# Turning the last unit's results sooner, and issuing the last store from ScalarE

## The chip, the cores and the metric

The kernel runs on one core of one Trainium2 chip. The metric is the device time of one execution in microseconds (us), median of the runs. Besides the times there is one profiled execution with a trace of every engine: TensorE (PE, with its weight loads as PEld), VectorE (DVE), ScalarE (ACT), GpSimd (POOL) and SyncE (SP), which issues most of the DMAs. L1656 means line 1656 of the kernel.

## What is computed

One layer of a streaming encoder, for 512 prompt frames and 64 sample frames together (576 rows, 2048 wide). The attention and convolution parts do not bear on the change. It ends with a gated feed-forward block:

```python
def hybrid_layer(x, ...):
    hn = rmsnorm(x, g_norm1)
    proj = hn @ w_in
...
    x = x + mix @ w_out
    h2 = rmsnorm(x, g_norm2)
    x = x + (jax.nn.silu(h2 @ w_gate) * (h2 @ w_up)) @ w_down
    return x, k, v, new_conv
```

The change lies in the last lines' product with `w_down` (5632 x 2048): in how its last result leaves the core.

## The kernel before

**Layout.** Activations are kept with channels on the 128 partitions and the 576 frames along the free axis, in two halves of 288 frames (`HALVES`). The outputs are wanted frame by frame, so every result block (128 channels x 288 frames) is turned before it is stored.

**Products.** Each float32 matrix is split into a high and a low part in the type fp32r, and a product is three matmuls. The large products are cut 2 x 2 and computed by seven block products (numbers 1 to 7 in `run`) in place of eight. A *unit* is one such set. One pair of input blocks, three matmuls, is one *step*: after each step `pipe.tick()` is called.

**Pipeline.** Side work is written as Python generators and handed to a small heap (`Pipeline`). `yield 9` in a worker means that it goes on nine steps later. A worker that is spawned after a product first runs at the next step, so `yield 9` ahead of the work puts it ten steps behind the addition. In the down projection the order of the instructions of all engines is kept as the program text gives it (`manual_schedule`, lines 119 and 1677).

**Down units.** `DOWN` lists 37 units. The last one (number `NU - 1`) treats columns 4 of 8 (d = 4) and four pairs, so each of its products is 4 steps, 12 matmuls. Its products come in the order 1, 2, 6, 7, 5, 4, 3. Four result blocks `acc[d, c, i]` are finished by them (c: which 128 columns, i: which half of the frames):

- acc 21045 (c 0, i 0) after product 2: ScalarE copies a partial sum (L428), VectorE adds the product (L450), GpSimd adds the partial sum (L452).
- acc 21048 (c 1, i 1) after product 5: ScalarE copies (L428), GpSimd adds (L452).
- acc 21047 (c 1, i 0) after product 4: VectorE adds (L450).
- acc 21046 (c 0, i 1) after product 3, the last one: VectorE adds (L450).

**Stores.** For all units but the last, `store_blocks` turns the block on VectorE in 32 x 32 tiles (L1607) and stores it in four to six DMAs from SyncE (L1613, L1615). For the last unit `store_y` has a worker: three transposes on TensorE into a PSUM bank `pot` (L1644; `misc` gives two banks in turn), two copies back on ScalarE (L1647 for 256 frames, L1653 for the other 32), then the stores: for the first half of the frames one DMA from SyncE (L1656), for the second half an L1635 for each 128 frames, cut at frame 512 into L1635 and L1637 (prompt and sample output). The last 32 frames go out from GpSimd.

**Lanes.** The program's framework gives every DMA of SyncE or ScalarE one of eight counting semaphores, DMAHW0 to DMAHW7, here called lanes. They are given out in turn, in the framework's own order of the instructions. A DMA adds 16 to its lane when it has landed, and before it is issued its engine waits until the lane has the count that all earlier users of that lane leave behind. An engine's DMAs are issued in its program order.

Of the kernel before, what the change touches and what calls it, by code (L numbers as in the profile page):

```python
# [16 lines left out]
P = 128  # L17
TP = 512
# [84 lines left out]
def tile_hybrid_stream_step(  # L103
# [6 lines left out]
    nc = tc.nc  # L110
# [5 lines left out]
    yp, ys = y_prompt[0], y_sample[0]  # L116
# [24 lines left out]
    def misc(name):  # L141
        return ps_z.tile([P, 512], F32, tag="misc", name=name, bufs=2)
# [99 lines left out]
    rows = {}  # L242
# [1298 lines left out]
    first, last = {v[0] for v in visits.values()}, {v[-1] for v in visits.values()}  # L1541
# [55 lines left out]
    def store_blocks(n, c, i):  # L1597
        d = UNITS[n][1]
        src, c0, f0 = acc[d, c, i], (2 * d + c) * P, HALVES[i][0]
        n_p = min(HALF, TP - f0)  # L1600

        def work():
            yield 9
            if not spare:
                spare.extend(down["pool"].tile([P, HALF], F32, tag=f"ob{k}", name="ob") for k in range(2))
            ob = spare.pop(0)
            nc.vector.transpose(out=ob, in_=src)  # L1607
            spare.append(src)
            yield 5
            for k in range(P // BK):  # L1610
                rows = ob[k * BK : (k + 1) * BK, :n_p].rearrange("j (t c) -> j t c", c=BK)
                cg = slice(c0 + k * BK, c0 + (k + 1) * BK)
                nc.sync.dma_start(out=yp[f0 : f0 + n_p, cg].rearrange("(t j) c -> j t c", j=BK), in_=rows)  # L1613
            for a in range(n_p, HALF, BK):
                nc.sync.dma_start(out=ys[a - n_p : a - n_p + BK, c0 : c0 + P].rearrange("j (g c) -> g j c", c=BK),  # L1615
                                  in_=ob[:, a : a + BK])

        pipe.spawn(work())
# [3 lines left out]
    def store_y(n, c, i):  # L1622
        if n < NU - 1:
            store_blocks(n, c, i)
            return

        d = UNITS[n][1]
        src, cs, f0 = acc[d, c, i], slice((2 * d + c) * P, (2 * d + c + 1) * P), HALVES[i][0]
        r = HALF - 2 * P

        def put(f, ap, queue=nc.sync):

            rows, n_p = ap.shape[0], max(min(TP - f, ap.shape[0]), 0)
            if n_p:
                queue.dma_start(out=yp[f : f + n_p, cs], in_=ap[:n_p])  # L1635
            if n_p < rows:
                queue.dma_start(out=ys[f + n_p - TP : f + rows - TP, cs], in_=ap[n_p:])  # L1637

        def work():
            yield 9  # L1640
            po = misc("pot")[:, : 3 * P]
            for q in range(3):
                w = min(P, HALF - q * P)
                nc.tensor.transpose(po[:w, q * P : (q + 1) * P], src[:, q * P : q * P + w], ident)  # L1644
            yield 3
            ob = src[:, : 2 * P].rearrange("p (i c) -> p i c", c=P)
            nc.scalar.copy(out=ob, in_=po[:, : 2 * P].rearrange("p (i c) -> p i c", c=P))  # L1647
            if len(rests) % 2 == 0:
                rests.append(spare.pop(0))
            else:  # L1650
                rests.append(rests[-1])
            obs = rests[-1][:r, : P] if len(rests) % 2 else rests[-1][:r, P : 2 * P]
            nc.scalar.copy(out=obs, in_=po[:r, 2 * P :])  # L1653
            yield 4
            if i == 0:
                nc.sync.dma_start(out=yp[: 2 * P, cs].rearrange("(i p) c -> p i c", p=P), in_=ob)  # L1656
            else:
                put(f0, ob[:, 0, :])
                put(f0 + P, ob[:, 1, :])
            put(f0 + 2 * P, obs, nc.gpsimd if n == NU - 1 else nc.sync)  # L1660

        pipe.spawn(work())


# [80 lines left out]
```

## Time and profile before

| what | us |
|---|---|
| median of 3 runs | 2329.69 |
| lowest and highest | 2328.64, 2332.22 |
| the profiled execution's own time | 2329.59 |
| its span, first to last instruction | 2327.9 |
| PE busy | 2315.9 (99%) |
| DVE busy | 1956.4 (84%) |
| ACT busy | 1221.5 (52%) |
| POOL busy | 298.1 (13%) |
| start of the last DMA issue | 2325.38 |

Times in the trace count from the start of the span. The columns of a timeline are: start, duration, engine, line, operation, output<-input, how many, and in brackets how long the engine was idle before and what released it. A row may merge several instructions of one group; its duration then goes from the first start to the last end. SPq rows are DMA issues of SyncE: the time is that of the issue, not that of the transfer. Ends of matmuls are modelled.

### The profile page before, as it was taken

What the parts mean: (1) busy time and instruction counts of PE and PEld (TensorE: products, weight loads), DVE (VectorE), ACT (ScalarE), POOL (GpSimd) and SP (SyncE); (2) the same over time, 40 slices, a digit from 0 to 9 for tenths busy, and PEclk for the clock granted to TensorE, in tenths of its full rate; (3) what the DMA queues carried; (4) which work ended last, traced back from release to release, by engine and by line L of the source; (5) the groups of instructions that cost most, each with busy time, mean ns of one, the idle gap of its engine ahead of it and who ended that gap; (6) DMA issues with size and microseconds to landing.
All of it is one profiled execution on the core that took longest, in us unless ns stands there. A gap on an engine that the chain in (4) does not pass through costs nothing.

```text
span 2327.9 us, 43552 instructions
## 1 busy us (share of the span) xinstructions
PE 2315.9 (99%) x17432; PEld 2306.7 (99%) x17432; DVE 1956.4 (84%) x2871; ACT 1221.5 (52%) x2170; POOL 298.1 (13%) x374
## 2 busy tenths in 40 slices
PE   9999999999999999999999999999999999999999
PEld 8999999999999999999999999999999999999999
DVE  8889989897777898888888888888888777887897
ACT  8556656456887564444444444444444444444443
POOL 0211121110332320000000000000000002431222
PEclk9999999999999999999999999999999999999999
DMA  8444343546643454444444444345344936885654
GB/s 272 136 118 130 91 142 109 145 131 209 192 144 108 162 204 127 155 139 140 150 134 150 133 146 155 116 152 158 116 155 136 349 129 211 222 242 186 205 137 100
DMA packets 533770, 368.57 MB, mean 158 GB/s; under 512 B 70278, under 2 KB 518016, under 8 KB 533568
## 3 DMA queue, kind: packets, MB, share of 16 engines
q1 hardware_dynamic: 527072, 356.45, 48.9%
q0 software_dynamic: 6384, 9.21, 2.2%
q8 instruction: 136, 2.23, 0.4%
q14 instruction: 66, 0.54, 0.1%
q10 hardware_dynamic: 112, 0.14, 0.0%
HBM read 285.52 MB, written 80.23 MB: 157 GB/s over the span
## 4 chain that ended last, share of the span: by engine, by line
PE 93%; ACT 3%; DVE 2%; DMA 1%; issue 0%; POOL 0%; SPq 0%; POOLq 0%; ACTq 0%; DVEq 0%
PE psy L405 47%; PE psw L405 23%; PE psx L405 12%; PE pjo L224 6%; PE pj L691 1%; PE pjz L691 1%; PE psv L405 1%; PE pjm L691 1%; DMA raw_a<-in_w_down_dram 0%; ACT ph L228 0%; PE psx L556 0%; ACT whi L176 0%; DVE whl L229 0%; DMA raw_b<-in_w_down_dram 0%; DMA vtok<-v_dram 0%
## 5 line engine op out<-in xcount | busy, mean ns | idle before, releaser
L229 DVE TENSOR_TENSOR whl<-raw_a,whl 128x1024 fp32r<-128x1024 f32 (+4 forms) x384 | 432.8, 1128 | 55.0 <-ACT whl L228 53.4
L405 PE MATMUL psy<-t,whl 128*128 128x288 f32 x3000 | 447.2, 294 | 0.0
L228 ACT CAST whl<-raw_a 128x1024 fp32r<-128x1024 f32 (+4 forms) x384 | 360.0, 939 | 139.9 <-PE psx L405 45.3
L405 PE MATMUL psy<-h_s,whl 128*128 128x288 f32 x2766 | 416.4, 294 | 0.6 <-ACT part L428 0.6
L405 PEld LDWEIGHTS psy<-t,whl 128*128 128x128 f32 x3000 | 414.3, 188 | 0.0
L405 PE MATMUL psw<-t,whl 128*128 128x288 f32 x2688 | 388.9, 294 | 0.0
L405 PEld LDWEIGHTS psy<-h_s,whl 128*128 128x128 f32 x2766 | 383.1, 188 | 0.9 <-ACT part L428 0.8
L405 PEld LDWEIGHTS psw<-t,whl 128*128 128x128 f32 x2688 | 366.7, 188 | 0.0
L228 ACT CAST whl<-raw_b 128x1024 fp32r<-128x1024 f32 (+5 forms) x234 | 211.4, 905 | 209.9 <-issue 71.4
L229 DVE TENSOR_TENSOR whl<-raw_b,whl 128x1024 fp32r<-128x1024 f32 (+5 forms) x234 | 253.2, 1082 | 72.7 <-ACT whl L228 71.6
L428 ACT COPY part<-psy 128x288 f32<-128x288 f32 x309 | 123.2, 399 | 346.6 <-PE psy L405 343.2
L405 PE MATMUL psx<-h_s,whl 128*128 128x288 f32 x1164 | 170.2, 294 | 0.0
L228 ACT CAST whl<-s 128x1024 fp32r<-128x1024 f32 (+5 forms) x103 | 95.3, 925 | 123.5 <-PE psw L405 116.0
L405 PEld LDWEIGHTS psx<-h_s,whl 128*128 128x128 f32 x1164 | 159.6, 188 | 0.0
L405 PE MATMUL psy<-t12a,whl 128*128 128x288 f32 x1056 | 150.5, 295 | 0.0
L405 PE MATMUL psw<-t34a,whl 128*128 128x288 f32 x1056 | 150.4, 295 | 0.0
L405 PEld LDWEIGHTS psy<-t12a,whl 128*128 128x128 f32 x1056 | 143.3, 188 | 0.4 <-ACT part L428 0.2
L405 PEld LDWEIGHTS psw<-t34a,whl 128*128 128x128 f32 x1056 | 143.5, 188 | 0.0
L1454 POOL DMA_DIRECT2D hid_dram<-form x7 | 5.2, 738 | 951.7 <-DVE form L229 944.5
L229 DVE TENSOR_TENSOR whl<-s,whl 128x1024 fp32r<-128x1024 f32 (+5 forms) x103 | 110.4, 1071 | 19.2 <-ACT whl L228 18.2
L224 PE MATMUL pjo<-mixc,whi 128*128 128x288 f32 x512 | 119.0, 300 | 0.0
L224 PE MATMUL pjo<-mixa,whi 128*128 128x288 f32 x512 | 102.8, 296 | 0.0
(565 smaller groups left out, 3920.8 us busy)
## 6 DMA issues: line engine op xcount, KB each, us to landing
hid_dram<-form SPq DMA_DIRECT2D x147, 288.0 KB
raw_a<-in_w_in_dram SPq DMA_DIRECT2D x22, 1024.0 KB
raw_b<-in_w_in_dram SPq DMA_DIRECT2D x22, 1024.0 KB
raw_b<-in_w_gate_dram SPq DMA_DIRECT2D x22, 1024.0 KB
raw_b<-in_w_up_dram SPq DMA_DIRECT2D x22, 1024.0 KB
raw_a<-in_w_gate_dram SPq DMA_DIRECT2D x22, 1024.0 KB
raw_a<-in_w_up_dram SPq DMA_DIRECT2D x22, 1024.0 KB
h_s<-hid_dram SPq DMA_DIRECT2D x10, 2016.0 KB
```

Of the source, the lines that this page charges most:

```text
L224: mm(ps, w_[:, k, csl], x_[:, a:b], start=(k == 0 and n == 0), stop=(k == nk - 1 and n == 2))
L228: cast = nc.scalar.copy(out=hi, in_=src)
L229: (lo_eng or nc.vector).tensor_tensor(out=lo, in0=src, in1=hi.bitcast(F32), op=ALU.subtract)
L405: mm(ps, whl[:, w_, j, :], x_, start=(start and j == 0 and q == 0), stop=(j == len(xs_) - 1 and q == 2), skip_group_check=True)
L428: nc.scalar.copy(out=t, in_=st["y"])
L691: mm(banks_[c][i], w3[:, kt % 8, c * P : (c + 1) * P], t[:, x_, :], start=(kt == 0 and n == 0), stop=(kt == KD - 1 and n == 2))
L1454: q.dma_start(out=hid_dram[fp][2 * n - 2 : 2 * n].rearrange("f p t -> p f t"), in_=t.bitcast(F32))
```

## The change

In `store_y` the worker's three delays become shorter (nine, three and four steps become three, one and one). So the transposes come four steps behind the addition, one product, and not ten; the copies two steps behind the transposes; the stores two behind the copies. And for the blocks with i = 1, the DMA of L1637 that closes the 128 frames from f0 + 128 goes to ScalarE's queue where c = 0, which is acc 21046, the last block of all.

```diff
-        def put(f, ap, queue=nc.sync):
+        def put(f, ap, queue=nc.sync, last=None):
 
             rows, n_p = ap.shape[0], max(min(TP - f, ap.shape[0]), 0)
             if n_p:
                 queue.dma_start(out=yp[f : f + n_p, cs], in_=ap[:n_p])
             if n_p < rows:
-                queue.dma_start(out=ys[f + n_p - TP : f + rows - TP, cs], in_=ap[n_p:])
+                (last or queue).dma_start(out=ys[f + n_p - TP : f + rows - TP, cs], in_=ap[n_p:])
 
         def work():
-            yield 9
+            yield 3
             po = misc("pot")[:, : 3 * P]
...
-            yield 3
+            yield 1
             ob = src[:, : 2 * P].rearrange("p (i c) -> p i c", c=P)
...
-            yield 4
+            yield 1
             if i == 0:
                 nc.sync.dma_start(out=yp[: 2 * P, cs].rearrange("(i p) c -> p i c", p=P), in_=ob)
             else:
                 put(f0, ob[:, 0, :])
-                put(f0 + P, ob[:, 1, :])
+                put(f0 + P, ob[:, 1, :], last=nc.scalar if c == 0 else nc.sync)
             put(f0 + 2 * P, obs, nc.gpsimd if n == NU - 1 else nc.sync)
```

TensorE, around products 7 and 5 of the last unit (psw is 7, psy is 5; pot 21045 are the transposes of the first block):

```order
-L405 MATMUL psw<-t_10084,whl 128x288 x3
-L405 MATMUL psw<-h_s_8772,whl 128x288 x3
-L405 MATMUL psw<-t_6_9981,whl 128x288 x3
-L405 MATMUL psw<-h_s_8771,whl 128x288 x3
-L405 MATMUL psy<-t_10084,whl 128x288 x3
-L405 MATMUL psy<-h_s_8772,whl 128x288 x3
 L1644 MATMUL pot<-ident,acc_21045 128x128 x2
 L1644 MATMUL pot<-ident,acc_21045 32x128
```

The block 21045 was turned in the middle of product 5; now its three transposes stand ahead of product 7, right behind product 6. In the same way those of 21048 move from behind product 3 to ahead of it. Those of 21047 and 21046 stay behind product 3.

SyncE, near the end of its program, before the change, with the lane (and engine) that each issue waits for; acc5 are blocks of column pair 5, acc2_20721 blocks of pair 7, the unit before the last:

```order
L1613 DMA out_0_dram<-acc5_21201 32x9x32 [waits DMAHW4_49]
L1613 DMA out_0_dram<-acc5_21201 32x9x32 [waits DMAHW5_49]
L1613 DMA out_0_dram<-acc5_21201 32x9x32 [waits DMAHW6_49]
L1613 DMA out_0_dram<-acc5_21202 32x7x32 [waits DMAHW7_49,DVE_49]
L1613 DMA out_0_dram<-acc5_21202 32x7x32 [waits DMAHW0_49]
L1613 DMA out_0_dram<-acc5_21202 32x7x32 [waits DMAHW1_49]
L1613 DMA out_0_dram<-acc5_21202 32x7x32 [waits DMAHW2_49]
L1615 DMA out_1_dram<-acc5_21202 4x32x32 [waits DMAHW3_49]
L1615 DMA out_1_dram<-acc5_21202 4x32x32 [waits DMAHW4_49]
L1613 DMA out_0_dram<-acc2_20721 32x7x32 [waits DMAHW5_49,DVE_49]
```

The same place now:

```order
L1613 DMA out_0_dram<-acc5_21201 32x9x32 [waits DMAHW4_49]
L1613 DMA out_0_dram<-acc5_21201 32x9x32 [waits DMAHW6_49]
L1613 DMA out_0_dram<-acc5_21201 32x9x32 [waits DMAHW7_49]
L1613 DMA out_0_dram<-acc5_21202 32x7x32 [waits DMAHW0_49,DVE_49]
L1613 DMA out_0_dram<-acc5_21202 32x7x32 [waits DMAHW1_49]
L1613 DMA out_0_dram<-acc5_21202 32x7x32 [waits DMAHW2_49]
L1613 DMA out_0_dram<-acc5_21202 32x7x32 [waits DMAHW3_49]
L1615 DMA out_1_dram<-acc5_21202 4x32x32 [waits DMAHW4_49]
L1615 DMA out_1_dram<-acc5_21202 4x32x32 [waits DMAHW5_49]
L1656 DMA out_0_dram<-acc4_21045 128x2x128 [waits DMAHW6_49,Activation_49]
```

Between the first two rows lane 5 is left out on SyncE, every later row has the next lane, and the store of 21045 (L1656) stands ten rows earlier than it did, ahead of the ten stores of pair 7. Behind the L1656 row stand 16 more issues, unchanged in order but for the last L1637, which has gone.

ScalarE, the end of its program now:

```order
L1647 COPY acc4_21047<-pot_26066 128x256 [waits DVE_49,PE_49]
L1653 COPY acc2_20721<-pot_26066 32x128
L1647 COPY acc4_21046<-pot_26075 128x256 [waits DVE_49,PE_49]
L1653 COPY acc2_20721<-pot_26075 32x128
L1637 DMA out_1_dram<-acc4_21046 32x128 [waits DMAHW5_49,Activation_49]
```

The last row is new, and it holds the lane 5 that SyncE left out. In the built program the counts on this lane are: the SyncE issue of L1615 for acc5_21200 leaves 1504; the ScalarE store waits for 1504 and leaves 1520; the second L1615 for acc5_21202 on SyncE (the last row but one above) waits for 1520 and leaves 1536. Before, the lane's users were all SyncE's, in SyncE's order.

## The prediction

> **What bounds the kernel now.** First the page: span, busy shares, shares of the chain of waits.
>
> ```profile
> span 2327.9 us, 43552 instructions
> PE 2315.9 (99%) x17432; PEld 2306.7 (99%) x17432; DVE 1956.4 (84%) x2871; ACT 1221.5 (52%) x2170; POOL 298.1 (13%) x374
> PE 93%; ACT 3%; DVE 2%; DMA 1%; issue 0%; POOL 0%; SPq 0%; POOLq 0%; ACTq 0%; DVEq 0%
> ```
>
> TensorE is the bound nearly everywhere. The change leaves the amount of work as it is and touches only the last 15 us, so the page decides nothing more. Next the chain of waits from 2316 us on, which shows what the end hangs on:
>
> ```profile
> 2317.36 0.33 PE pot L1644 x3
> 2317.69 0.81 PE psy L405 x6
> 2318.49 1.61 PE psw L405 x12
> 2320.11 1.59 PE psy L405 x12
> 2321.70 0.34 PE pot L1644 x3
> ...
> 2324.14 0.52 POOLq L1741
> ```
>
> The products run without a gap to 2321.70, where product 3 ends; behind it come the transposes. The chain is drawn through GpSimd's queue, but a later thing stands in the timeline of SyncE:
>
> ```profile
> 2314.60 1.13 SPq L1615 DMA_DIRECT2D out_dram<-acc  x2
> 2315.83 1.88 SPq L1613 DMA_DIRECT2D out_dram<-acc  x4
> 2317.75 1.13 SPq L1615 DMA_DIRECT2D out_dram<-acc  x2
> 2318.99 1.92 SPq L1613 DMA_DIRECT2D out_dram<-acc  x4
> 2321.00 0.40 SPq L1656 DMA_DIRECT2D out_dram<-acc  x1
> 2322.51 0.83 SPq L1635 DMA_DIRECT2D out_dram<-acc  x2
> 2323.40 0.41 SPq L1637 DMA_DIRECT2D out_dram<-acc  x1
> 2323.91 0.39 SPq L1656 DMA_DIRECT2D out_dram<-acc  x1
> 2324.40 0.92 SPq L1635 DMA_DIRECT2D out_dram<-acc  x2
> 2325.38 0.42 SPq L1637 DMA_DIRECT2D out_dram<-acc  x1
> ```
>
> From 2322.51 on SyncE issues one store after the other. The last issue begins at 2325.38, and 2327.9 - 2325.38 = **2.52 us** later the span is over: landing and the program's close. So the end is SyncE's last issue, and a change of the end is a change of that start.
>
> **The change part by part: TensorE.** Now the transposes of 21045 stand directly behind product 6, and they need GpSimd's addition to that block. From the timelines of TensorE (product 7 and two sets of transposes), GpSimd and VectorE:
>
> ```profile
> 2314.81 0.56 PE L405 MATMUL psw<-t,whl 128*128 128x288 f32 x3
> 2317.20 0.49 PE L1644 MATMUL pot<-ident,acc 128*128 128x128 f32 x3
> 2314.20 1.24 POOL L452 TENSOR_TENSOR acc<-acc,part 128x288 f32<-128x288 f32 x1 [5.52 <-DVE acc L450]
> 2319.06 0.81 POOL L452 TENSOR_TENSOR acc<-acc,part 128x288 f32<-128x288 f32 x1 [2.71 <-ACT part L428]
> 2322.69 0.55 PE L1644 MATMUL pot<-ident,acc 128*128 128x128 f32 x3 [0.34 <-ACT acc L1653]
> 2321.73 0.46 DVE L450 TENSOR_TENSOR acc<-psy,acc 128x288 f32<-128x288 f32 x1 [1.06 <-PE psy L405]
> ```
>
> The transposes could begin at 2314.81, but the addition ends at 2314.20 + 1.24 = 2315.44, and a step from one engine to another costs some 0.06 (below). So TensorE stands until 2315.50: **0.69 us lost**. GpSimd's spans are rough; with the 0.81 of its other row the loss is 2315.07 - 2314.81 = 0.26, and that is the lower end. Product 7, its partial sums and everything behind it on TensorE wait with it.
>
> For 21048 the same wait costs nothing: shifted alike, the addition ends at 2319.06 + 0.81 = 2319.87, against 2320.11 - 0.16 = 2319.95, where TensorE reaches the transposes (it starts them some 0.16 before the modelled end of the product, 2317.20 in the row above against 2317.36 in the chain). With the 1.24 of the other row 0.4 would be lost; upper end. The transposes of 21045 only move inside the stretch; those of 21048 come from behind product 3 to before it, 0.34. Product 3 now ends at 2321.70 + 0.69 + 0.34 = **2322.73**.
>
> ScalarE's two early copies cost nothing, since ScalarE is idle for 2.60 us where they fall (first row below). GpSimd's small store ahead of its last addition, half a microsecond, lies in the 2.71 idle of the row above.
>
> ```profile
> 2318.58 0.40 ACT L428 COPY part<-psy 128x288 f32<-128x288 f32 x1 [2.60 <-PE psy L405]
> 2322.38 0.25 ACT L1653 COPY acc<-pot 32x128 f32<-32x128 f32 x1
> 2323.27 0.37 ACT L1647 COPY acc<-pot 128x256 f32<-128x256 f32 x1 [0.21 <-PE pot L1644]
> 2323.54 0.25 ACT L1653 COPY acc<-pot 32x128 f32<-32x128 f32 x1
> ```
>
> Here is the 0.06: the copy that ends at 2322.38 + 0.25 = 2322.63 releases TensorE at 2322.69. Now for the last block, 21046. VectorE's addition starts 0.03 behind product 3 and takes 0.46: 2323.22. Before, the transposes of 21048 and 21047 covered it; now those of 21047 alone lie beside it, so the last transposes begin at 2323.28. ScalarE's L1647 starts 0.58 after them (2322.69 to 2323.27): 2323.86. L1653 starts 0.27 later, ends after 0.25: 2324.38. ScalarE's new store is queued behind it and is issued at about **2324.43**.
>
> **SyncE.** The lanes decide this. The rows of the order in the section on the change show SyncE's second L1615 of acc5_21202 waiting on lane 5 for a count that only ScalarE's last store brings. SyncE issues in order. Before, this L1615 was the second issue of the row at 2314.60; nothing on it waited for the end of the kernel. Now SyncE stands there from about 2315.2, and behind it wait 17 more issues: two L1656, eight L1613, two L1615, four L1635 and one L1637. No engine waits for these, so TensorE still finishes; but the program cannot end without them.
>
> ScalarE's store must land first. For SyncE's and ScalarE's issues the trace has no landing times, for GpSimd's stores of the same 16 KB to the same outputs it has. The group of all issues to the outputs from 2300 us on:
>
> ```profile
> L1613 SPq DMA_DIRECT2D out_dram<-acc x26: 316/444/1566, 2299.7 to 2320.4; - x26
> L1637 POOL DMA_DIRECT2D out_dram<-acc x2: 498/510/523, 2322.9 to 2324.2; - x2
> DMA to landing us min/median/max: 1.7/1.8/2.0
> ```
>
> I take the median, 1.8. It cannot be shorter than the issue itself (0.42, the row at 2325.38) nor longer than the 2.52 from SyncE's last issue to the end. So the lane is free at 2324.43 + 1.8 = 2326.23, and SyncE goes on at 2326.29. The Trainium skill, page "DMA: Bandwidth & Descriptors", section "Specifications", gives a first-byte latency of about 0.6 us for DMAs issued by SyncE or ScalarE and about 1 us for GpSimd's. An estimate by it puts the landing 0.4 us sooner and the sum at 2338.8; no run here shows it yet.
>
> Then 18 issues in a row, 17 distances from start to start, taken from SyncE's rows above:
>
> - three L1615 at (2318.99 - 2317.75) / 2 = 0.62: 1.86
> - eight L1613: (2317.75 - 2315.83) + (2321.00 - 2318.99) = 1.92 + 2.01 = 3.93
> - two L1656 at 2324.40 - 2323.91 = 0.49: 0.98
> - two L1635 and one L1637: 2323.91 - 2322.51 = 1.40
> - the first of the last two L1635: 0.48, half of 2325.38 - 2324.40 rounded down
>
> That is **8.65 us**. The last issue starts at 2326.29 + 8.65 = 2334.94 instead of 2325.38. With the close of 2.52 the span is 2337.46, and with 2329.59 - 2327.9 = 1.69 around it the execution takes 2339.15. The profiled execution of before took 2329.59, 0.1 below the median of 2329.69, so nothing is added: **2339.2 us**, 9.5 us or 0.4% more.
>
> The distances have bounds as well: the quickest L1613 of the group took 0.32 and the median 0.44, and one took 1.57. If two of eighteen are held up like that one, 2.2 is added; if they all go at the better L1613 distance of 0.48, 17 x 0.48 = 8.16, 0.5 is saved.
>
> **The rivals.** *First, not slower: SyncE doesn't stand.* This is what the edit reads like: results turned sooner, one issue fewer on SyncE. Place: the L1615 that waits on lane 5. If it passes at 2315.2, L1656 of 21045 waits for ScalarE's copy (transposes at 2315.50, copy 2316.08 to 2316.45), is issued at 2316.50, and the ten stores of pair 7 take until 2316.99 + 1.92 + 1.24 + 2.01 = 2322.16. The three of 21048 follow until 2323.56, L1656 of 21047 until 2324.05; the first L1635 of 21046 waits for its copy, 2323.86 + 0.37 = 2324.23, and the second starts at 2324.74. That is 0.64 before 2325.38: 2329.0 us, within 0.2%, so not slower. SyncE's idle time between 2321.40 and 2322.51 is used up, but TensorE's 0.69 is lost. For it speak only the rows of before, where no lane held SyncE up near the end; against it the order of the lane's users, which is fixed. It decides on when the lane opens: the result is slower by more than 0.2% (4.7 us) as soon as SyncE gets past that row later than 2325.38 + 4.7 - 8.65 = 2321.4, and ScalarE cannot issue before product 3 has ended at 2322.73.
>
> The Trainium skill has a rule for this rival: on the page "DMA: Bandwidth & Descriptors", section "Issuing engines are not separate DMA queues", DMAs begun on several engines run on the same DMA engines, and this saves only the time that the sequencer takes to issue. By that rule the move would be worth one issue on SyncE and cost nothing, as this rival has it; the trace of before has that issue at 0.42.
>
> *Second, slower still: the backlog is held up.* The 18 issues come at once, and each waits for its lane's user eight issues before. At 0.5 an issue that leaves 4 us, well over 1.8, so the lanes should not bind. But the L1613 of 1.57 in the group above shows that an issue can be held up for 1.1 for a reason that the rows do not name. Two such: 2339.15 + 2.2 = 2341.4.
>
> *Third, the lane frees sooner or later than by GpSimd's landing.* With 0.42 the time is 2337.8, with 2.52 it is 2339.9; this belongs to the forecast.
>
> **How the numbers follow.** SyncE standing with the backlog at its usual pace: 0.81. The backlog held up: 0.13. SyncE not standing: 0.06, of which 0.01 for a gain over 0.2%, which no row here supports. Low end: all the savings together, 0.43 on TensorE, 1.38 on landing and 0.5 on pace, 2339.15 - 2.3 = 2336.9. High end: 0.4 on the second wait, 0.7 on landing and one hold-up of 1.1 give 2341.4, and the second rival ends there too; the three runs of before lie up to 2.5 above their median, but a median moves less, and I stop at 2341.8. The first rival, 0.06, is left out. About 0.2%, 4.7 us, is what a measurement of this kernel can tell from no change. So slower 0.94, within 0.2% 0.05, faster 0.01.
>
> **What would show it.** In the timeline of SyncE of the changed kernel: the first L1615 of the pair at about 2314.6 and then no issue until about 2326.3, then 18 issues to about 2335. In that of ScalarE: a DMA issue at about 2324.4. In that of TensorE: a wait of 0.3 to 0.7 for GpSimd ahead of the transposes of 21045 at about 2315, none ahead of those of 21048, product 3 ending near 2322.7. In the page: everything before 2314 as it was. The prediction is wrong if SyncE issues L1656 near 2316.5, or if ScalarE's store goes out before product 3 has ended.

## The result and the profile after

The changed kernel takes 2339.11 us, median of 6 runs (2338.56 to 2341.69), against 2329.26 us (2328.61 to 2332.22, 6 runs) before: a ratio of 1.0043, 95% interval 1.0033 to 1.0053. It is slower. The profiled execution took 2339.02 us with a span of 2337.2.

One name first: in the notes on the kernel, in the prediction and in one expectation below the blocks acc2_20721 are called blocks of column pair 7. They are those of pair 2; the last unit but one treats pair 2. No number hangs on it.

The page after, three of its first lines (the last one is TensorE's busy share in 40 equal slices, in tenths):

```profile
span 2337.2 us, 43552 instructions
PE 2316.1 (99%) x17432; PEld 2307.2 (99%) x17432; DVE 1955.2 (84%) x2871; ACT 1221.5 (52%) x2170; POOL 298.7 (13%) x374
...
PE   9999999999999999999999999999999999999997
```

Busy times are those of before within a few tenths of a per cent, and the number of instructions is the same; the span is 9.3 longer. So something waits. The timeline of SyncE's issues after, from 2312 us on:

```profile
2312.72 1.78 SPq L1613 DMA_DIRECT2D out_dram<-acc  x4
2314.55 11.82 SPq L1615 DMA_DIRECT2D out_dram<-acc  x2
2326.47 0.41 SPq L1656 DMA_DIRECT2D out_dram<-acc  x1
2326.98 1.91 SPq L1613 DMA_DIRECT2D out_dram<-acc  x4
2328.93 1.13 SPq L1615 DMA_DIRECT2D out_dram<-acc  x2
2330.17 1.91 SPq L1613 DMA_DIRECT2D out_dram<-acc  x4
2332.18 0.87 SPq L1635 DMA_DIRECT2D out_dram<-acc  x2
2333.09 0.42 SPq L1637 DMA_DIRECT2D out_dram<-acc  x1
2333.61 0.39 SPq L1656 DMA_DIRECT2D out_dram<-acc  x1
2334.10 0.91 SPq L1635 DMA_DIRECT2D out_dram<-acc  x2
```

Two L1615 in one merged row of 11.82 us, where before they took 1.13: the second is held up. The same timeline cut to that one issue and to the last one, then SyncE's waits (what, for whom, in total, times, longest) and the end of ScalarE's timeline:

```profile
2325.82 0.54 SPq L1615 DMA_DIRECT2D out_dram<-acc  x1
...
2334.57 0.45 SPq L1635 DMA_DIRECT2D out_dram<-acc  x1
```

```profile
SPq L1615 <- DMA out_dram<-acc: 10.7, 1, 10.7
```

```profile
2323.92 0.37 ACT L1647 COPY acc<-pot 128x256 f32<-128x256 f32 x1 [0.31 <-PE pot L1644]
2324.19 0.25 ACT L1653 COPY acc<-pot 32x128 f32<-32x128 f32 x1
2324.32 0.34 ACTq L1637 DMA_DIRECT2D out_dram<-acc  x1
```

SyncE waits 10.7 us for a store to land, and goes on 1.50 us after ScalarE's store was issued at 2324.32. The records of the trace name that store: the sixteenth increment on ScalarE's lane comes at 2325.81, and SyncE's issue starts at 2325.82. All 18 issues that were left then go out one after the other, with every other engine done. The page says the same: TensorE's busy share in the last of the 40 slices has fallen from 9 to 7.

### The profile page after: what moved, and what is told of

It reads as the page before. It is cut to its first block, busy times and chain, and to the rows that moved or that the text cites. A ratio compares the mean times of both kernels' runs of the same rounds, so it can differ in the third digit from the quotient of the medians.

```text
span 2337.2 us, 43552 instructions
## 1 busy us (share of the span) xinstructions
PE 2316.1 (99%) x17432; PEld 2307.2 (99%) x17432; DVE 1955.2 (84%) x2871; ACT 1221.5 (52%) x2170; POOL 298.7 (13%) x374
## 4 chain that ended last, share of the span: by engine, by line
PE 93%; ACT 3%; DVE 2%; DMA 1%; issue 1%; POOL 0%; SPq 0%; POOLq 0%; ACTq 0%; DVEq 0%
PE psy L405 46%; PE psw L405 23%; PE psx L405 12%; PE pjo L224 6%; PE pj L691 1%; PE pjz L691 1%; PE psv L405 1%; PE pjm L691 1%; DVE whl L229 0%; ACT ph L228 0%; PE psx L556 0%; DMA raw_b<-in_w_down_dram 0%; ACT whi L176 0%; DMA vtok<-v_dram 0%; DVE hbe L229 0%
## 5 line engine op out<-in xcount | busy, mean ns | idle before, releaser
L228 ACT CAST whl<-raw_a 128x1024 fp32r<-128x1024 f32 (+4 forms) x384 | 360.1, 939 | 140.0 <-PE psx L405 44.0
L228 ACT CAST whl<-raw_b 128x1024 fp32r<-128x1024 f32 (+5 forms) x234 | 211.4, 905 | 210.4 <-issue 71.4
L228 ACT CAST whl<-s 128x1024 fp32r<-128x1024 f32 (+5 forms) x103 | 95.3, 926 | 123.3 <-PE psw L405 116.0
```

What stands on the lines that cost most here:

```text
L228: cast = nc.scalar.copy(out=hi, in_=src)
```

## The experiments

The theory under test is that of the lane: SyncE issues in order, one of its issues waits for a count that only ScalarE's last store brings, and all that stands behind it is added after the kernel's own end. Rivals: the shorter delays make the loss (TensorE's new wait for GpSimd, and the store of 21045 put ahead of ten others), or a store from ScalarE at the very end is slow of itself.

Profiles of different kernels are shifted against each other by up to 1.7 us before the change's place is reached, with the same instructions up to there (but for the order of four stores of each block in the two kernels called "lane in order"). So ends are also given from a common mark, the start of a cast on ScalarE (L228), 0.2 us into product 6 and ahead of everything that the edits move (2313.42 in the timeline of before, 2313.36 after):

```profile
2313.36 0.62 ACT L228 CAST whl<-raw_a 128x512 fp32r<-128x512 f32 x1 [0.91 <-PE psx L405]
```

| kernel | time, us | ratio to before, 95% interval | mark | span | span - mark |
|---|---|---|---|---|---|
| before | 2329.26 | | 2313.42 | 2327.9 | 14.48 |
| the change | 2339.11 | 1.0043 (1.0033 to 1.0053) | 2313.36 | 2337.2 | 23.84 |
| delays only | 2329.82 | 1.0001 (0.9991 to 1.0010) | 2314.27 | 2328.9 | 14.63 |
| queue only | 2339.07 | 1.0037 (1.0024 to 1.0051) | 2314.29 | 2337.6 | 23.31 |
| another block on ScalarE | 2336.95 | 1.0031 (1.0019 to 1.0043) | 2313.98 | 2335.9 | 21.92 |
| lane in order | 2329.76 | 1.0000 (0.9991 to 1.0010) | 2313.72 | 2328.3 | 14.58 |
| fewer behind | 2333.52 | 1.0019 (1.0010 to 1.0028) | 2313.74 | 2332.5 | 18.76 |
| last store on GpSimd | 2329.84 | 1.0003 (0.9994 to 1.0012) | 2312.59 | 2327.6 | 15.01 |
| lane in order, five steps | 2328.68 | 0.9998 (0.9990 to 1.0007) | 2312.89 | 2326.8 | 13.91 |

Ratios are against runs of before on the same chip (medians 2329.76 for the first four experiments, 2329.54 for the last three). The last three columns come from one profiled execution of each kernel, so their differences have no interval.

**The delays alone.**

```diff
-                put(f0 + P, ob[:, 1, :], last=nc.scalar if c == 0 else nc.sync)
+                put(f0 + P, ob[:, 1, :])
```

> The three shorter delays as in the change, but the last store stays on SyncE, so no lane has a ScalarE store among SyncE's. Theory of the lane: SyncE doesn't stand; its first L1656 is issued near 2316.5 and its last store starts at about 2325.3, so 2329.5 us, within 0.1% of before. Rival 'delays' (TensorE's wait for GpSimd and the store of 21045 put ahead of ten others make the loss): about 2339, as with the whole change. Rival 'ScalarE's queue' (a store from ScalarE at the end is slow of itself): about 2329.5, as the lane says.

Measured: 2329.82, no difference. SyncE doesn't stand for long; the issue ahead of the ten stores is at 2317.36, 3.09 behind the mark (expected 2316.5, that is 3.08 behind the mark of before).

```profile
2315.46 1.13 SPq L1615 DMA_DIRECT2D out_dram<-acc  x2
2317.36 0.40 SPq L1656 DMA_DIRECT2D out_dram<-acc  x1
...
2326.10 0.42 SPq L1637 DMA_DIRECT2D out_dram<-acc  x1
```

The delays do not make the loss.

**The queue alone.** The three delays of before, the last store on ScalarE:

```diff
-            yield 3
+            yield 9
             po = misc("pot")[:, : 3 * P]
...
-            yield 1
+            yield 3
...
-            yield 1
+            yield 4
```

> The delays of before, the last store on ScalarE. In the built program SyncE's second L1615 of acc5_21202 again waits for the count that the ScalarE store leaves, with 17 issues behind it. Theory of the lane: the ScalarE store starts at about 2323.9, SyncE goes on 1.5 later at 2325.4, its last issue starts 8.7 later at 2334.1, so 2338.5 us, 0.5 below the whole change. Rival 'delays': 2329.3, since the delays are those of before. Rival 'ScalarE's queue': 2338 to 2339 as well, but SyncE's rows then don't stand from 2315 on.

Measured: 2339.07, the whole loss; from the mark 0.53 less than the change, against 0.5 expected. In its timeline of SyncE:

```profile
2315.49 11.26 SPq L1615 DMA_DIRECT2D out_dram<-acc  x2
2326.85 1.88 SPq L1613 DMA_DIRECT2D out_dram<-acc  x4
```

The second of the two L1615 by itself, and ScalarE's store:

```profile
2326.21 0.54 SPq L1615 DMA_DIRECT2D out_dram<-acc  x1
```

```profile
2324.50 0.34 ACTq L1637 DMA_DIRECT2D out_dram<-acc  x1
```

The order of the stores is that of before, L1656 behind the ten; still the second L1615 is held up, for 10.2 us. This leaves the store on ScalarE, but not yet whether by its lane or of itself.

**Another block on ScalarE.**

```diff
-                put(f0 + P, ob[:, 1, :], last=nc.scalar if c == 0 else nc.sync)
+                put(f0 + P, ob[:, 1, :], last=nc.scalar if c == 1 else nc.sync)
```

> As the change, but the ScalarE store is the L1637 of block 21048 (c 1), which is done some 2.5 us sooner; the last L1637 is back on SyncE. In the built program the row of SyncE that waits for it is the fourth L1613 of acc5_21202, two rows earlier, so 20 issues stand. Theory of the lane: store at 2321.8, landed and seen at 2323.3, 19 distances of together 9.8, last issue at 2333.1, so 2337.5 us, 1.6 below the change, and the stand of SyncE ends about 2.5 us sooner. Rival 'ScalarE's queue at the end': the last store is SyncE's as before, so 2329.5. Rival 'delays': 2339 as with the change.

Measured: 2336.95, expected 2337.5. ScalarE's store, and the row of SyncE that it holds up (now an L1613), with the last issue:

```profile
2322.21 0.34 ACTq L1637 DMA_DIRECT2D out_dram<-acc  x1
```

```profile
2323.72 0.32 SPq L1613 DMA_DIRECT2D out_dram<-acc  x1
```

```profile
2333.43 0.42 SPq L1637 DMA_DIRECT2D out_dram<-acc  x1
```

The store is no longer the last thing, and SyncE's last issue is an ordinary one 11 us later; yet the kernel is slow. SyncE goes on 1.51 after ScalarE's issue, as in the change (1.50), and 2.72 sooner from the mark (9.74 against 12.46). That a ScalarE store is slow at the very end cannot give this.

**Lane in order.** The whole change with ScalarE's store, but the last copy goes to a buffer that the last stores of the unit before have read, and the four L1613 of every block of the other units go out in reverse order:

```diff
+            turned7.append(ob)
             yield 5
-            for k in range(P // BK):
+            for k in reversed(range(P // BK)):
...
+            if (c, i) == (0, 1):
+                obs = turned7[-1][:r, :P]
             nc.scalar.copy(out=obs, in_=po[:r, 2 * P :])
```

> The whole change, ScalarE store included, but the last 32 frames of 21046 are copied into the buffer from which the last stores of pair 7 were sent (and these four go out in reverse order). So the copy waits for SyncE's last L1613, the framework orders the ScalarE store behind it, and no row of SyncE waits for a count of the ScalarE store. Theory of the lane: SyncE doesn't stand, its last issue starts near 2324.8, ScalarE's store at about 2324.3 to 2324.6, so 2329.0 us, within 0.1% of before. Rivals 'delays' and 'ScalarE's queue': 2339, since both the delays and the store from ScalarE are still there.

Measured: 2329.76, the median of before. The ScalarE store is there (2324.65), the delays are there, only the count that SyncE's row waits for is now SyncE's own:

```profile
2314.92 1.13 SPq L1617 DMA_DIRECT2D out_dram<-acc  x2
2316.82 0.39 SPq L1660 DMA_DIRECT2D out_dram<-acc  x1
...
2324.64 0.82 SPq L1637 DMA_DIRECT2D out_dram<-acc  x2
```

```profile
2324.65 0.36 ACTq L1639 DMA_DIRECT2D out_dram<-acc  x1
```

(Lines are some two to four higher in this kernel: L1617 is the old L1615.) Both rivals fall here: with the delays and ScalarE's store of the change, and only a buffer and the order of some stores altered so that the lane's users come in order, the loss is gone.

**Fewer issues behind.**

```diff
             yield 5
+            if d == 2 and (c, i) in ((0, 1), (1, 0)):
+                return
             for k in range(P // BK):
```

> The whole change, but the ten stores of the last two blocks of the unit before the last (eight L1613, two L1615) are left out, so those output columns are not written for these frames. The lanes are as in the change up to there: SyncE's second L1615 of acc5_21202 waits for the ScalarE store, but only 7 issues stand behind it in place of 17. Theory of the lane: SyncE goes on at the same time as in the change, and the ten issues less take 1.95 + 1.24 + 2.01 = 5.2 off the end: 2339.1 - 5.2 = 2333.9 us. Rival 'ScalarE's queue' or 'delays' (the loss is not the backlog behind the lane): 2338 to 2339, since those stores then lie beside other work.

Measured: 2333.52, expected 2333.9. SyncE's held-up issue in this kernel:

```profile
2326.19 0.54 SPq L1617 DMA_DIRECT2D out_dram<-acc  x1
```

From the mark it starts at the same time as in the change (12.45 against 12.46), and the end comes 5.08 sooner, with ten issues less, against 5.2 expected. So every issue that stands behind the lane is paid for, at about 0.51 each. The rest of the price stays: with seven issues behind, the end is still 4.28 later than before (18.76 against 14.48).

**Last store on GpSimd.**

```diff
-                put(f0 + P, ob[:, 1, :], last=nc.scalar if c == 0 else nc.sync)
+                put(f0 + P, ob[:, 1, :], last=nc.gpsimd if c == 0 else nc.sync)
```

> The change, but the last L1637 goes to GpSimd's queue, whose DMAs have semaphores of their own, and not to ScalarE's. No row of SyncE waits for it. Theory of the lane: within 0.1% of before; GpSimd has one issue of 0.5 more at its end, and since the runs without the lane wait end some 3.2 us after GpSimd's last issue, about 2330.3 us against 2329.8 before. Rival 'delays': 2339. Rival 'ScalarE's queue': as the lane.

Measured: 2329.84, no difference that can be told; from the mark 0.53 more than before, against 0.5 expected. A queue with semaphores of its own does not hold SyncE up. The last two issues of GpSimd:

```profile
2323.90 1.07 POOL L1637 DMA_DIRECT2D out_dram<-acc  x2 [0.27 <-ACT acc L1653]
```

**Lane in order, five steps.** As the lane in order, with

```diff
-            yield 3
+            yield 5
             po = misc("pot")[:, : 3 * P]
```

> The lane in order as in the run before with the shared buffer, and the first delay five steps in place of three: the transposes of 21045 stand two steps into product 7, where GpSimd's addition is done. Expected: no wait of TensorE ahead of them (it was 0.5 us), so product 3 and the last copies come some 0.65 sooner against the products before them than with three steps, GpSimd's last store as well, and the time is 2329.2 against 2329.8 before. By the other reading, that the hold on TensorE was hidden, the time is that of three steps, 2329.8. The difference is below what the timing can tell; the trace tells it.

Measured: 2328.68 against 2329.54, a ratio whose interval holds 1, so the timing can't tell it from before; from the mark it is 0.57 shorter than before and 0.67 shorter than with three steps. TensorE's rows with three steps (lane in order) and with five, around the first transposes:

```profile
2315.78 0.55 PE L1646 MATMUL pot<-ident,acc 128*128 128x128 f32 x3 [0.51 <-POOL acc L452]
```

```profile
2314.68 0.56 PE L405 MATMUL psw<-h_s,whl 128*128 128x288 f32 x3
2315.08 0.49 PE L1646 MATMUL pot<-ident,acc 128*128 128x128 f32 x3
```

With five steps there is no wait. In these two traces GpSimd's last store is issued 0.70 sooner from the mark with five steps (10.71 against 11.41), and the span ends 0.67 sooner. So the hold on TensorE, forecast at 0.69, was worth its size at the end, where no lane is in the way; the times cannot confirm it.

## Why the prediction was right, point by point

The mechanism, the place and the size were right: 2339.2 forecast, 2339.11 measured, range 2336.9 to 2341.8; as a difference, 9.5 us forecast and 9.85 measured. That the sum came within 0.13 of the profiled execution (2339.15 against 2339.02) is in part luck, since two errors in it cancel (below). Its steps against the trace after:

- **TensorE's hold.** Forecast 0.69, at least 0.26. The transposes start at 2315.41, 2.05 behind the mark, against 2.08 forecast; the row gives 0.51 of idle time, since the idle time is counted from the modelled end of the matmuls (2314.34 + 0.56 = 2314.90), not from where the next could have started, some 0.40 behind 2314.34. From there it is 0.67.

```profile
2315.41 0.55 PE L1644 MATMUL pot<-ident,acc 128*128 128x128 f32 x3 [0.51 <-POOL acc L452]
2320.60 0.49 PE L1644 MATMUL pot<-ident,acc 128*128 128x128 f32 x3
2322.56 0.49 PE L1644 MATMUL pot<-ident,acc 128*128 128x128 f32 x3
2323.36 0.52 PE L1644 MATMUL pot<-ident,acc 128*128 128x128 f32 x3 [0.31 <-DVE acc L450]
```

- **The second wait, for 21048.** Forecast none; the row at 2320.60 has none.
- **ScalarE's store.** Forecast 2324.43, found at 2324.32.
- **Landing.** Forecast 1.8 from GpSimd's stores, found 1.50 until SyncE goes on (1.51, 1.50 and 1.71 in three experiments). This is the term that was off most: 0.36 too long, SyncE's step of 0.06 included. It was sized from GpSimd's stores because the views give SyncE's and ScalarE's stores no landing; the records of the trace do, and before the change SyncE's last store of 16 KB landed 1.55 after its issue (2325.38 to 2326.93). GpSimd's stores of L1637 landed in 1.7 after the change. The estimate by the Trainium skill, page "DMA: Bandwidth & Descriptors", section "Specifications", 0.4 less than GpSimd's, came nearer in the change (1.4 and the step, 1.46), but not in the kernel with the queue alone (1.71).

```profile
DMA to landing us min/median/max: 1.7/1.7/1.7
```

- **The backlog.** Forecast 8.65 from the first to the last of 18 issues, found 2334.57 - 2325.82 = 8.75. Nothing like the 1.57 us issue came, so the second rival did not happen.
- **The close.** Forecast 2.52 and 1.69 around the span, found 2337.2 - 2334.57 = 2.63 and 1.82. These and the backlog together are 0.34 longer than forecast, and make up for the shorter landing.

The first rival, SyncE not standing, was 2329.0, a gain of 0.6. Its mechanism could be tried by itself (lane in order): there SyncE's last issue, 2324.64 + 0.82 - 0.41 = 2325.05, does come 11.33 behind the mark and not 11.96, the 0.63 of the working. But the kernel was not faster, 14.58 against 14.48. The step that failed in it is one sentence at the start: that the end is SyncE's last issue. It was so before, but not once that issue came sooner. The end of GpSimd's timeline before, and in the lane in order with three steps and with five:

```profile
2324.16 0.50 POOL L1637 DMA_DIRECT2D out_dram<-acc  x1 [0.20 <-issue]
```

```profile
2325.13 0.50 POOL L1639 DMA_DIRECT2D out_dram<-acc  x1 [0.41 <-ACT acc L1657]
```

```profile
2323.60 0.50 POOL L1639 DMA_DIRECT2D out_dram<-acc  x1 [0.41 <-ACT acc L1657]
```

GpSimd's last store waits for the last copy, which the hold on TensorE and the transposes ahead of product 3 put off by 0.67. The span ends 3.17 (lane in order), 3.18 (delays only: 2325.72 to 2328.9), 3.20 (five steps) and 3.13 us (last store on GpSimd: the later of its two, about 2324.47, to 2327.6) after GpSimd's last issue, and 3.74 after it before. So in these four runs the distances point to GpSimd's store as the last thing, and the close of the program shows it. There SyncE passes twelve semaphore instructions (at L1741, L1745 with the shared buffer); by the records of the trace GpSimd's last stores are waited for first, the lanes behind them. These instructions and the waits in them, before:

```profile
L1741 SPq EVENT_SEMAPHORE  x12: 17/28/28, 2326.2 to 2327.8; - x12
SPq L1741 <- DMA out_dram<-acc: 0.6, 2, 0.4
```

In the lane in order, with the landing of GpSimd's last store:

```profile
L1745 SPq EVENT_SEMAPHORE  x12: 17/28/28, 2326.9 to 2328.3; - x12
SPq L1745 <- DMA out_dram<-acc: 1.4, 1, 1.4
DMA to landing us min/median/max: 1.8/1.8/1.8
```

In the lane in order SyncE waits once for a store, until GpSimd's has landed (2325.13 + 1.8 = 2326.93), and 1.4 later the span is over; it is 1.4 as well with the delays only (2327.5 to 2328.9), with five steps (2325.4 to 2326.8) and with the last store on GpSimd (2326.2 to 2327.6). Before, it waited twice: until GpSimd's store had landed at 2326.2, 1.7 before the end, and once more behind that, for its own last store. So a sooner last issue of SyncE could have gained some 0.3 at most (an estimate, 1.7 less 1.4), not the 0.6 of the working; and as GpSimd's store came later, that went too.

By the Trainium skill, page "DMA: Bandwidth & Descriptors", section "Issuing engines are not separate DMA queues", starting DMAs on several engines saves only issue time. The runs agree where the lane is in order, with a ratio of 1.0000. What the change cost, 9.4 us from the mark, comes from the order in which the program's counting semaphores are used.

## What to carry to other kernels

Before a DMA is moved to another engine's queue, look at what the other issues on its semaphore wait for: where a framework hands out a few counting semaphores in its own order, an in-order queue can stand still until a store has landed that another engine issues last. The order of the built program shows it without a run, as a lane that is left out in one queue and turns up in another. The new end is the landing of that store plus every issue that stands behind it, so it is worked out from issue distances; and when one last thing is made sooner, look for the next one before counting the gain.

## What the runs showed of the hardware

With nothing else running, SyncE's stores of 16 to 128 KB went out at 0.46 to 0.62 us each (means of the rows of one line), about the distances that they had beside TensorE's work; 18 took 8.75 us from the first start to the last, 8.65 by the distances of before. ScalarE's stores of 16 KB let SyncE go on 1.50 to 1.71 us after their issue, in four kernels. The granted TensorE clock, 1.00 up to 2314 us, is 0.58 in the idle stretch at the end of the changed kernel (columns: stretch, its length, busy time and number of PE, PEld, DVE, ACT and POOL instructions, granted clock, DMA share, GB/s), which is enough for its mean of 0.998 (10.80 x 0.42 / 2337.2 = 0.002); no matmul runs there.

```profile
2326.40:2337.20 10.80, 0.00 (x0) 0.00 (x0) 0.00 (x0) 0.00 (x0) 0.00 (x0) 0.58 0.34 76
```
